# Heads turned from channel rows to token rows by VectorE squares of 32 and transfers through DRAM, in both layers

## The chip, the core and the metric

The program runs on one core of a Trainium2 chip. The metric is the device time of one execution in microseconds (us); before the change it is 2276.68 us, the median of three runs (2275.68 to 2278.51). The engines are TensorE (PE, and PEld for its weight loads), VectorE (DVE), ScalarE (ACT), GpSimd (POOL) and SyncE (SP), which here issues every transfer (DMA).

## What is computed

One step of a two-layer decoder for a prompt of 1024 tokens and for 8 sample tokens. Layer 0 has 8 gated DeltaNet heads and 8 mLSTM heads, layer 1 has 4 GLA heads and 4 retention heads. Cut to what matters:

```python
def _even_mixer(h, ...):                       # layer 0
    proj = h @ w_in
    u_conv = causal_conv(u_a); q_a, k_a, v_a = split(silu(u_conv))
    q_a, k_a = _l2n(q_a) * DK_A ** -0.5, _l2n(k_a)
    o_a, new_gdn = _gated_delta(q_a, k_a, v_a, beta, g_a, s_gdn)   # S_new = e^last S + k^T (e^(last-b) U)
    h_b, ... = _mlstm(q_b, k_b, v_b, ig, fg, ...)                  # C_new = se C + (k we)^T v
    h_b = sigmoid(o_pre) * _rms(h_b, mlstm_norm_w)
    y = concat([_rms(o_a), h_b]) * silu(z)
    return y @ w_out, ...

def _odd_mixer(h, ...):                        # layer 1
    o_c, new_gla = _gla(q_c, k_c, v_c, g_c, s_gla)                 # o += att @ v
    o_d, new_ret = _retention(rotary(q_d), rotary(k_d), v_d, s_ret)
    y = concat([_rms(o_c), _rms(o_d)]) * silu(z)
    return y @ w_out, ...
```

The projections give every head with its channels in the partitions and the 1024 tokens along the row. A product that sums over tokens, such as the state's update, needs its operands with tokens in the partitions. Turning them is what this case is about.

## The kernel before, in words

The prompt is cut into 8 chunks of 128 tokens. A projection of 128 columns (`proj`) multiplies the weights, split into a high and a low part (`whi`, `wlo`), with the input, split likewise (tiles `s_h`), in 72 passes of 344 columns into three PSUM banks `pj`. Weights are loaded into one of two buffers `wf` (512 KB each), ScalarE writes `whi`, and VectorE or GpSimd writes `wlo`. The out projections at the end of each layer first split the 16 rows of `y` in the same way, through the staging tiles `s_pt` and `s_u`, into tiles that the layer's last heads leave free; two late rows (14 and 15) come last in the sums.

Everything is recorded first and then put in order by `Recorder.order`, a planner: it takes each operation's cost and dependences from formulas in the code (`_cost`, `_pe_cost`) and writes one fixed order for every engine and for SP's issues. So an edit to one helper moves instructions everywhere. All operations have the same source line in the profile (L448, where the planner emits them), and groups are told apart by the names of their tiles.

In layer 0 a DeltaNet head (`gdn_mix`) waits for `k2`, `v2` and `q2`, which `conv_silu` makes in this order from three projections. Before the change it turns `k2` by eight TensorE transposes into two PSUM banks (`transpose4`), from which ScalarE takes squares (tile `N`, whose row sums normalise the keys) and VectorE the decayed keys `kd`. It turns `v2` likewise into `vs`. Then come the matrix `N` (products of `k2` with itself), its inverse (tiles `EM`, `Y`, with round trips through the DRAM tiles `nd` and `yd`), and a chain over the 8 chunks, in which `kd` and `vs` are read. `k2`, `kd`, `vs` and `N` have one buffer each. An mLSTM pair (`mlstm_pair_mix`) turns `mk` into `kwe`, an mLSTM head (`mlstm_mix`) turns its value `v` (in one of three buffers `pt`) into `va`, and `mlstm_out` turns the normalised output `hn` (tile `mp`) back. Transposes are 128 x 128, in groups of four to a bank.

In layer 1 both kinds of heads turn two values of 128 channels in `v_tokens`, by `by_token`: sixteen VectorE transposes each of 32 partitions by 256 elements, which need neither TensorE nor a transfer. `by_token` also turns the keys there.

## Time and profile before

| | |
|---|---|
| median of three runs | 2276.68 us |
| the profiled execution | 2275.8 us, of which the span from the first to the last instruction is 2273.7 us |
| TensorE matmuls | 2206.5 us busy, 97% of the span |
| VectorE | 1379.6 us, 61% |
| ScalarE | 745.8 us, 33% |
| GpSimd | 604.7 us, 27% |
| transfers | 236.10 MB, 104 GB/s on average |

Busy time is a union, so overlapped instructions count once. The mean duration of a matmul is that of one from its issue to its modelled end; neighbours overlap, and the time that a matmul holds TensorE is the step from its start to the start of the next one. Layer 0's heads run from about 150 to 1165 us of the span, its out projection to about 1330 us, layer 1's heads to about 2050 us.

### The profile page before, as it was taken

To read this page: it belongs to the slowest core of one execution; us is meant where nothing else is said; L and a number is where in the kernel's file an instruction comes from. 1 tells how busy PE (TensorE), PEld (TensorE's weight loads), DVE (VectorE), ACT (ScalarE), POOL (GpSimd) and SP (SyncE) were. 2 spreads that over 40 slices of the span, in tenths; PEclk is the share of its full clock that TensorE was granted. 3 is DMA by queue.
4 is the path that set the end of the run, shared out by engine and by line. 5 is a ranking of instruction groups with operands and counts; after the bars stand their busy time and mean duration, and the time that the engine had idled before them with its cause. 6 is when DMAs were issued, how large, how long until landed. Compare 5 with 4: busy or idle time off the path is not lost.

```text
span 2273.7 us, 42794 instructions
## 1 busy us (share of the span) xinstructions
PE 2206.5 (97%) x17820; PEld 2056.0 (90%) x17820; DVE 1379.6 (61%) x2771; ACT 745.8 (33%) x1374; POOL 604.7 (27%) x409
## 2 busy tenths in 40 slices
PE   6989999999999999999989999999999999998998
PEld 4867788899998999899989999999999999998997
DVE  6764646566475746647452356785885885886322
ACT  4422323232233223232331134234225324334322
POOL 3221211212123102221330032533532642643210
PEclk9999999999999999999999999999999999999999
DMA  9363453523133223433273221233143143155212
GB/s 261 122 150 81 144 151 83 162 53 93 46 111 103 76 60 87 103 95 84 93 221 93 75 86 38 59 122 104 49 133 96 48 134 104 45 170 191 75 56 94
DMA packets 285944, 236.10 MB, mean 104 GB/s; under 512 B 47803, under 2 KB 258229, under 8 KB 285742
## 3 DMA queue, kind: packets, MB, share of 16 engines
q1 hardware_dynamic: 285750, 233.37, 35.7%
q8 instruction: 140, 2.29, 0.4%
q14 instruction: 54, 0.44, 0.1%
HBM read 186.35 MB, written 47.18 MB: 103 GB/s over the span
## 4 chain that ended last, share of the span: by engine, by line
PE 87%; DVE 5%; DMA 5%; issue 1%; SPq 1%; ACT 1%; POOL 0%; POOLq 0%; DVEq 0%; ACTq 0%
PE pj L448 68%; PE A L448 14%; PE B L448 5%; SPq L448 1%; DMA wf<-in_ev_w_in 1%; DMA wf<-in_ada_w 1%; DMA yd<-s_EM 1%; DVE wlo L448 1%; DMA s_h<-in_x_prompt 1%; DVE s_EM L448 0%; DVE arena L448 0%; DVE s_N L448 0%; DVE s_tmp L448 0%; DMA s_EM<-yd 0%; DVE s_zz L448 0%
## 5 line engine op out<-in xcount | busy, mean ns | idle before, releaser
L448 PE MATMUL pj<-s_h,whi 128*128 128x344 f32 (+1 forms) x6024 | 1498.6, 327 | 9.8 <-ACT whi L448 3.8
L448 PEld LDWEIGHTS pj<-s_h,whi 128*128 128x128 f32 (+1 forms) x6024 | 1043.6, 189 | 40.5 <-issue 22.9
L448 PE MATMUL pj<-s_h,wlo 128*128 128x344 f32 (+1 forms) x3024 | 985.0, 326 | 0.3 <-DVE wlo L448 0.3
L448 PEld LDWEIGHTS pj<-s_h,wlo 128*128 128x128 f32 (+1 forms) x3024 | 571.2, 189 | 19.5 <-issue 15.4
L448 DVE TENSOR_TENSOR wlo<-wf,whi 128x1024 fp32r<-128x1024 f32 x112 | 145.7, 1301 | 259.3 <-ACT whi L448 235.9
L448 ACT ACTIVATE whi<-wf 128x1024 fp32r<-128x1024 f32 (+1 forms) x146 | 152.3, 1043 | 380.3 <-PE pj L448 308.9
L448 ACT ACTIVATE s_pt<-pj 128x344 f32<-128x344 f32 (+1 forms) x170 | 77.0, 453 | 276.0 <-PE pj L448 271.5
L448 POOL TENSOR_TENSOR wlo<-wf,whi 128x1024 fp32r<-128x1024 f32 (+1 forms) x32 | 79.9, 2497 | 179.8 <-ACT whi L448 179.8
L448 POOL TENSOR_TENSOR arena<-arena,base 128x8 f32<-128x8 f32 (+5 forms) x38 | 59.9, 1580 | 240.1 <-DVE arena L448 240.1
L448 POOL TENSOR_TENSOR s_tmp<-s_EM 128x512 f32<-128x512 f32 (+1 forms) x60 | 91.6, 1540 | 100.3 <-DVE s_N L448 32.1
L448 DVE SCALAR_TENSOR_TENSOR arena<-arena,A 128x128 f32<-128x128 f32 (+1 forms) x84 | 32.9, 391 | 111.3 <-PE A L448 111.2
L448 DVE SCALAR_TENSOR_TENSOR s_pt<-s_u,base,s_pt 128x1024 f32<-128x1024 f32 x72 | 96.7, 1343 | 0.5
L448 ACT ACTIVATE s_u<-pj 128x344 f32<-128x344 f32 x93 | 41.6, 452 | 140.6 <-PE pj L448 70.7
L448 POOL TENSOR_TENSOR s_tmp<-s_tmp,arena 128x1024 f32<-128x1024 f32 (+2 forms) x26 | 46.7, 1808 | 124.9 <-PE A L448 66.0
L448 DVE SCALAR_TENSOR_TENSOR s_zz<-s_pt,pj 128x344 f32<-128x344 f32 x96 | 48.5, 505 | 24.4 <-ACT s_pt L448 23.5
L448 DVE SCALAR_TENSOR_TENSOR arena<-arena,B 64x130 f32<-64x130 f32 (+1 forms) x84 | 31.1, 370 | 51.0 <-PE B L448 49.9
L448 POOL TENSOR_TENSOR s_kd<-s_kd,s_vs 128x1032 f32<-128x1032 f32 x8 | 19.3, 2411 | 160.0 <-ACT s_vs L448 142.8
L448 ACT ACTIVATE arena<-A,arena 128x128 f32<-128x128 f32 x64 | 23.4, 366 | 107.3 <-PE A L448 107.3
L448 DVE STREAM_TRANSPOSE s_kd<-s_u 32x256 f32<-32x256 f32 x128 | 55.8, 436 | 3.9 <-ACT s_u L448 1.7
L448 POOL MEMSET s_u<- 128x3 f32 x24 | 2.4, 100 | 206.8 <-DVE s_pt L448 197.5
L448 DVE TENSOR_TENSOR s_EM<-s_EM 64x15 f32<-64x15 f32 (+7 forms) x240 | 49.2, 205 | 13.5 <-DMA s_EM<-nd 7.7
L448 DVE STREAM_TRANSPOSE s_vs<-s_v 32x256 f32<-32x256 f32 x128 | 55.7, 435 | 1.9
(643 smaller groups left out, 3665.7 us busy)
## 6 DMA issues: line engine op xcount, KB each, us to landing
wf<-in_ev_w_in SPq DMA_DIRECT2D x64, 512.0 KB
wf<-in_od_w_in SPq DMA_DIRECT2D x48, 512.0 KB
wf<-in_ada_w SPq DMA_DIRECT2D x32, 512.0 KB
s_pt<-yd SPq DMA_DIRECT2D x24, 516.0 KB
s_tmp<-sd SPq DMA_DIRECT2D x24, 512.0 KB
yd<-s_qg SPq DMA_DIRECT2D x15, 516.0 KB
wf<-in_ev_w_out SPq DMA_DIRECT2D x14, 512.0 KB
wf<-in_od_w_out SPq DMA_DIRECT2D x14, 512.0 KB
```

Source lines behind the costliest of these rows:

```text
L448: op.fn(*[self.placed(x) for x in op.args], **{k: self.placed(x) for k, x in op.kw.items()})
```

## The change

A new helper `squares(y, x, z)` turns a head. One VectorE transpose turns all squares of 32 by 32 of the 128 x 1024 tile at once and writes them into a scratch tile `y`; one transfer writes that to one of four DRAM tiles `td` (512 KB); four transfers, one for each group of 32 partitions, read it back into a tile `z` in pieces of 256 elements, so that each square lands in its place. The result is a view of `z` whose elements stand in another order in the row, and the operation that follows puts them in order as it reads.

In layer 0 this takes the place of every `transpose4` and of the transposes in `mlstm_out`: twice for each DeltaNet head, once for each mLSTM pair, twice for each mLSTM head, 36 times in all. The operations behind it read SBUF where they read PSUM: one multiply of 1024 elements for `kd` and for `vs` instead of two of 512, one ScalarE square and one ScalarE copy (`va`) of 1024, four fused multiplies of 256 in `mlstm_out` instead of two of 512. In layer 1 `v_tokens` calls `squares` for its 16 values, followed by a ScalarE copy; the keys there stay with `by_token`. The planner's cost of a VectorE transpose becomes a function of its size.

```diff
-    def transpose4(self, src, g):
-        p = self.ps()
-        for c in range(4):
-            o = 512 * g + 128 * c
-            self.tr(p[:, 128 * c:128 * c + 128], src[:, o:o + 128])
-        return p
...
+        ksq = self.squares(kd.rearrange("p c d -> p (c d)"), k2, self.slot("N", name="ksq"))
+        V.tensor_tensor(in_4(kd), ksq, by_c(self.g_kdec[:, :, h]), op=ALU.mult)
+        self.act(ksq, ksq, AF.Square)
...
+        z = self.squares(vs.rearrange("p c d -> p (c d)"), v2, v2)
+        V.tensor_tensor(in_4(vs), z, by_c(kk[:, 2, :]), op=ALU.mult)
...
+        z = self.squares(kwe.rearrange("p c x d -> p (c x d)"), self.mk, qs)
...
+        z = self.squares(va.rearrange("p c d -> p (c d)"), v, v)
         G.memset(va[:, :, 128:130], 1.0)
-        for g in range(2):
-            t = self.transpose4(v, g)
-            self.act(va[:, 4 * g:4 * g + 4, 0:128], t.rearrange("p (c d) -> p c d", d=128), AF.Copy)
+        self.act(va[:, :, 0:128].rearrange("p c (a j) -> p c a j", j=32), z, AF.Copy)
...
+        z = self.squares(self.slot("va", name="ht"), hn, hn)
+        y4 = y[:, 0:T].rearrange("p (c a j) -> p c a j", c=NC, a=4)
+        for i in range(4):
+            V.scalar_tensor_tensor(y4[:, :, i, :], z[:, :, i, :], self.nw[:, 1:2], y4[:, :, i, :], op0=ALU.mult,
+                                   op1=ALU.mult)
...
+    def squares(self, y, x, z):
+        dma = self.nc.sync.dma_start
+        y, z = y[:, 0:T], z[:, 0:T]
+        self.nc.vector.transpose(y.rearrange("p (b c j) -> p b c j", b=4, c=NC),
+                                 x[:, 0:T].rearrange("p (c b i) -> p b c i", b=4, c=NC))
+        d = self.td[self.turn("td", 4)]
+        dma(d, y)
+        for b in range(4):
+            dma(z[32 * b:32 * b + 32].rearrange("i (a x) -> i a x", a=4),
+                d.rearrange("(a i) (b x) -> b i a x", a=4, b=4)[b])
+        return z.rearrange("p (a c j) -> p c a j", a=4, c=NC)
+
     def v_tokens(self, v):
...
-            t = self.slot(tag, [128, NC, 128], name="vt")
-            self.by_token(t, v[i])
-            vt.append(t)
+            t = self.slot(tag, name="vt")
+            z = self.squares(t, v[i], v[i])
+            self.act(t[:, 0:T].rearrange("p (c a j) -> p c a j", c=NC, a=4), z, AF.Copy)
```

How the order moves, at three places. First TensorE in layer 0, as DeltaNet head 3 begins: `pj` rows are projections, `A_...<-base,s_k` and `A_...<-base,s_v` are transposes of `k2` and `v2` (with the identity, in `base`). Before:

```order
L448 MATMUL pj_111<-s_h_723,whi_107 128x344
L448 MATMUL pj_111<-s_h_703,wlo_109 128x344
L448 MATMUL A_113<-base,s_k_63 128x128 x4
L448 MATMUL A_114<-base,s_k_63 128x128 x4
L448 MATMUL A_115<-base,s_v_65 128x128 x4
L448 MATMUL pj_112<-s_h_443,whi_106 128x344
```

Here twelve transposes stand between two banks of a projection. The same place in the changed kernel, where `A_...<-s_k` is the product of `k2` with itself:

```order
L448 MATMUL pj_111<-s_h_727,whi_107 128x344
L448 MATMUL pj_111<-s_h_707,wlo_109 128x344
L448 MATMUL A_113<-s_k_63 128x128
L448 MATMUL A_114<-s_k_63 128x128
L448 MATMUL A_115<-s_k_63 128x128
L448 MATMUL pj_112<-s_h_447,whi_106 128x344
```

The transposes are gone, and products that stood behind them have moved up. In the whole program TensorE's order has 14434 matmuls before and 14146 after, 288 fewer (288 = 36 times 8).

Second SP, which issues transfers in order, between the end of DeltaNet head 2 (its state is stored to `out_p_gdn`) and the middle of head 3; `wf` are weight loads. Before:

```order
L448 DMA out_p_gdn<-arena 128x128
L448 DMA out_p_conv<-arena 3x128
L448 DMA out_s_conv<-arena 8x128
L448 DMA wf_104<-in_ev_w_in 128x8x128
L448 DMA out_p_mc<-arena 64x128
L448 DMA out_p_mn<-arena 64x1
L448 DMA wf_105<-in_ada_w 128x1024
L448 DMA wf_104<-in_ada_w 128x1024
L448 DMA wf_105<-in_ev_w_in 128x8x128
```

A weight load stands here behind short stores alone. The same place in the changed kernel:

```order
L448 DMA out_p_gdn<-arena 128x128
L448 DMA td_129<-s_kd_66 128x1024
L448 DMA wf_104<-in_ev_w_in 128x8x128
L448 DMA rd_128<-s_Y_72 4x258
L448 DMA wf_105<-in_ada_w 128x1024
L448 DMA arena<-in_state_gdn_conv 24x128
L448 DMA out_p_conv<-arena 3x128
L448 DMA out_s_conv<-arena 8x128
L448 DMA s_N_70<-td_129 32x4x256 x4
L448 DMA s_Y_72<-rd_128 128x1032
L448 DMA wf_105<-in_ev_w_in 128x8x128
```

One weight load now stands behind the write of a square, which waits for VectorE's transpose, and one behind the four reads, which wait for that write to land.

Third VectorE, where layer 1's last head meets the out projection: `s_zz<-s_pt,pj` finish the last two projections, `s_mq<-s_pt,s_EM` and `s_va<-s_pt,s_mk` are low parts of rows of `y`, which the out projection needs. Before:

```order
L448 STREAM_TRANSPOSE s_kd_12163<-s_u_79 32x8x32 x7
L448 SCALAR_TENSOR_TENSOR s_zz_10696<-s_pt_83,pj_110 128x344
L448 STREAM_TRANSPOSE s_kd_12163<-s_u_79 32x8x32 x4
L448 TENSOR_TENSOR wlo_109<-wf_105,whi_107 128x1024
L448 SCALAR_TENSOR_TENSOR s_zz_10696<-s_pt_83,pj_111 128x344
...
L448 STREAM_TRANSPOSE s_vs_12426<-s_v_12191 32x8x32 x8
L448 SCALAR_TENSOR_TENSOR s_zz_81<-s_pt_84,pj_111 128x344
L448 STREAM_TRANSPOSE s_vs_12426<-s_v_12191 32x8x32
L448 TENSOR_TENSOR s_aT_11683<-B_117,arena 128x512
L448 TENSOR_TENSOR s_mq_18166<-s_pt_82,s_EM_18105 128x1032
```

The first low part stands behind the small transposes and behind the last piece of the last projection. In the changed kernel:

```order
L448 TENSOR_TENSOR s_mq_17736<-s_pt_82,s_EM_17725 128x1032
L448 STREAM_TRANSPOSE s_vs_12190<-s_v_12094 128x1024
L448 STREAM_TRANSPOSE s_kd_12069<-s_u_79 128x1024
L448 SCALAR_TENSOR_TENSOR s_zz_10604<-s_pt_83,pj_112 128x344
L448 SCALAR_TENSOR_TENSOR s_zz_10604<-s_pt_83,pj_110 128x344
L448 TENSOR_TENSOR s_va_17803<-s_pt_82,s_mk_17792 128x1032
L448 TENSOR_TENSOR wlo_109<-wf_105,whi_107 128x1024
L448 SCALAR_TENSOR_TENSOR s_zz_10604<-s_pt_83,pj_111 128x344
L448 SCALAR_TENSOR_TENSOR s_zz_81<-s_pt_84,pj_112 128x344
```

Two large transposes stand where 32 small ones stood, and two low parts have moved ahead of the last projections' ends.

## Rows read from the trace of the kernel before

**Rows 1.** The page's busy time, share of the span and instructions of each engine

```profile
PE 2206.5 (97%) x17820; PEld 2056.0 (90%) x17820; DVE 1379.6 (61%) x2771; ACT 745.8 (33%) x1374; POOL 604.7 (27%) x409
```

**Rows 2.** The page's chain that ended last, shares of the span by engine

```profile
PE 87%; DVE 5%; DMA 5%; issue 1%; SPq 1%; ACT 1%; POOL 0%; POOLq 0%; DVEq 0%; ACTq 0%
```

**Rows 3.** Busy time by stretch; columns: length, PE, PEld, DVE, ACT, POOL, clock, DMA share, GB/s

```profile
150.00:1100.00 950.00, 935.58 (x7824) 851.43 (x7820) 565.43 (x1381) 280.06 (x583) 184.19 (x143) 1.00 0.36 96
...
1400.00:2000.00 600.00, 599.98 (x5562) 573.37 (x5561) 457.67 (x713) 220.46 (x340) 256.57 (x140) 1.00 0.30 89
2000.00:2100.00 100.00, 91.81 (x644) 87.85 (x643) 75.25 (x124) 43.23 (x61) 38.97 (x16) 0.95 0.56 187
...
2054.00:2065.00 11.00, 5.41 (x21) 4.91 (x21) 10.80 (x19) 5.94 (x7) 4.70 (x2) 0.53 0.70 231
```

**Rows 4.** Groups by form, TensorE transposes; columns: count, busy us, mean ns, idle

```profile
L448 PE MATMUL B<-base,s_mp 128*128 128x128 f32 x80 | 12.5, 277 | 0.0
...
L448 PE MATMUL B<-base,s_pt 128*128 128x128 f32 x64 | 9.7, 274 | 0.0
L448 PE MATMUL A<-base,s_v 128*128 128x128 f32 x64 | 9.6, 273 | 0.0
...
L448 PE MATMUL A<-base,s_k 128*128 128x128 f32 x64 | 8.6, 274 | 0.0
...
L448 PE MATMUL B<-base,s_mk 128*128 128x128 f32 x32 | 4.9, 272 | 0.0
```

**Rows 5.** Timeline of TensorE round five transposes; columns: start, duration, instruction, count

```profile
546.29 0.71 PE L448 MATMUL B<-base,s_pt 128*128 128x128 f32 x5
546.76 0.56 PE L448 MATMUL pj<-s_h,whi 128*128 128x344 f32 x2
547.16 0.32 PE L448 MATMUL pj<-s_h,wlo 128*128 128x344 f32 x1
547.32 0.48 PE L448 MATMUL pj<-s_h,whi 128*128 128x344 f32 x2
```

**Rows 6.** Groups by form, VectorE transposes; columns as in group 4

```profile
L448 DVE STREAM_TRANSPOSE s_vs<-s_v 32x256 f32<-32x256 f32 x128 | 55.7, 435 | 1.9
...
L448 DVE STREAM_TRANSPOSE s_EM<-s_EM 128x256 f32<-128x256 f32 x16 | 7.1, 442 | 10.5 <-DMA s_EM<-yd 10.3
```

**Rows 7.** A 512 KB read, issue and first use, and SP's waits for 512 KB writes

```profile
1111.37 0.33 SPq L448 DMA_DIRECT2D s_mp<-gd  x1
...
1115.04 2.49 POOL L448 TENSOR_TENSOR s_mp<-arena,s_mp 128x1024 f32<-128x1024 f32 x1 [1.52 <-DMA s_mp<-gd]
...
SPq L448 <- DMA out_s_gdn<-s_tmp: 9.5, 4, 3.4
```

**Rows 8.** Timeline of VectorE and TensorE, DeltaNet head 3

```profile
496.52 1.22 DVE L448 SCALAR_TENSOR_TENSOR s_k<-s_pt,s_pt 128x1032 f32<-128x1032 f32 x1
...
513.37 1.23 DVE L448 SCALAR_TENSOR_TENSOR s_q<-s_pt,s_pt 128x1032 f32<-128x1032 f32 x1 [1.21 <-ACT s_pt L448]
...
579.91 0.48 PE L448 MATMUL A<-arena,s_kd 128*128 128x128 f32 x2
```

**Rows 9.** Timeline of SP and ScalarE, one weight load and its use

```profile
597.58 0.38 SPq L448 DMA_DIRECT2D wf<-in_ev_w_in  x1
...
608.20 1.06 ACT L448 ACTIVATE whi<-wf 128x1024 fp32r<-128x1024 f32 x1 [3.16 <-PE pj L448]
```

**Rows 10.** TensorE's waits from 2000 to 2100 us, and VectorE there

```profile
PE pj L448 <- ACT s_mk L448: 3.6, 1, 3.6
PE pj L448 <- DVE s_va L448: 2.5, 1, 2.5
...
2042.52 3.58 DVE L448 STREAM_TRANSPOSE s_vs<-s_v 32x256 f32<-32x256 f32 x8
```

**Rows 11.** TensorE, transposes of the last mLSTM output and the first use of that row

```profile
1158.63 1.03 PE L448 MATMUL B<-base,s_mp 128*128 128x128 f32 x8
...
L448 PE MATMUL pj<-s_mp,s_zz x3: 318/320/322, 1208.2 to 1210.1; 128*128 128x344 f32 x3
```

More of the change, by code (lines that the diff above doesn't have):

```diff
@@ L116, in _cost @@
         if method == "transpose":
-            return 436.0, False
+            return 100 + 1.31 * n, False
         if method == "tensor_tensor_scan":
@@ L1218, in gdn_mix @@
         vs = self.slot("vs", [128, NC, L], name="vs")
-        for g in range(2):
-            p = self.transpose4(v2, g)
-            V.tensor_tensor(vs[:, 4 * g:4 * g + 4, :], p.rearrange("p (c d) -> p c d", d=L),
-                            kk[:, 2, 4 * g:4 * g + 4].unsqueeze(2).to_broadcast([128, 4, L]), op=ALU.mult)
+        z = self.squares(vs.rearrange("p c d -> p (c d)"), v2, v2)
+        V.tensor_tensor(in_4(vs), z, by_c(kk[:, 2, :]), op=ALU.mult)
         em = self.slot("EM", [128, NC, L], name="EM")
@@ L1435, in mlstm_pair_mix @@
         kwe = self.slot("kwe", [128, NC, 2, 64], name="kwe")
-        for g in range(2):
-            t = self.transpose4(self.mk, g).rearrange("p (c x d) -> p c x d", c=4, x=2)
-            for x in range(2):
-                V.tensor_tensor(kwe[:, 4 * g:4 * g + 4, x, :], t[:, :, x, :],
-                                self.g_we[:, 4 * g:4 * g + 4, 2 * p + x].unsqueeze(2).to_broadcast([128, 4, 64]),
-                                op=ALU.mult)
+        qs = self.slot("qs", [128, T], name="qs")
+        z = self.squares(kwe.rearrange("p c x d -> p (c x d)"), self.mk, qs)
+        for x in range(2):
+            V.tensor_tensor(kwe[:, :, x, :].rearrange("p c (a j) -> p c a j", j=32), z[:, :, 2 * x:2 * x + 2, :],
+                            self.g_we[:, :, 2 * p + x].unsqueeze(2).unsqueeze(3).to_broadcast([128, NC, 2, 32]),
+                            op=ALU.mult)
         self.kwe = kwe
-        qs = self.slot("qs", [128, T], name="qs")
         for x in range(2):
@@ L1478, in mlstm_mix @@
         va = self.slot("va", [128, NC, 130], name="va")
+        z = self.squares(va.rearrange("p c d -> p (c d)"), v, v)
         G.memset(va[:, :, 128:130], 1.0)
-        for g in range(2):
-            t = self.transpose4(v, g)
-            self.act(va[:, 4 * g:4 * g + 4, 0:128], t.rearrange("p (c d) -> p c d", d=128), AF.Copy)
+        self.act(va[:, :, 0:128].rearrange("p c (a j) -> p c a j", j=32), z, AF.Copy)
         V.tensor_copy(self.vs[:, x, :], v[:, T:W])
@@ L1541, in mlstm_out @@
         y = oz
-        for g in range(2):
-            t = self.ps()
-            for i in range(4):
-                self.tr(t[:, 128 * i:128 * i + 128], hn[:, 4 * g + i, :])
-            s = slice(512 * g, 512 * g + 512)
-            V.scalar_tensor_tensor(y[:, s], t, self.nw[:, 1:2], oz[:, s], op0=ALU.mult, op1=ALU.mult)
+        hn = hn.rearrange("p c d -> p (c d)")
+        z = self.squares(self.slot("va", name="ht"), hn, hn)
[3 more added lines that the diff above has]
+                                   op1=ALU.mult)
         V.tensor_copy(self.ozs[:, h % 2, :], oz[:, T:W])
@@ L1712, in v_tokens @@
         for i, tag in enumerate(("kd", "vs")):
-            t = self.slot(tag, [128, NC, 128], name="vt")
-            self.by_token(t, v[i])
-            vt.append(t)
+            t = self.slot(tag, name="vt")
+            z = self.squares(t, v[i], v[i])
+            self.act(t[:, 0:T].rearrange("p (c a j) -> p c a j", c=NC, a=4), z, AF.Copy)
+            vt.append(t[:, 0:T].rearrange("p (c d) -> p c d", c=NC))
         return vt
@@ L2142, in build @@
             self.rd = [dr.tile([4, QB], F32, name=f"rd{i}") for i in range(2)]
+            self.td = [dr.tile([128, T], F32, name=f"td{i}") for i in range(4)]
             self.nyd = {x: [dr.tile([64, 528], F32, name=f"{x}{i}") for i in range(2)] for x in ("nd", "yd")}
```

10 lines of the change are left out of this document (3 added, 7 removed).

## The prediction

> **What bounds the kernel now.** I read the page's busy shares first: TensorE is busy for 97% of the span, VectorE for 61%, ScalarE for 33%, GpSimd for 27% [rows 1]. Then the chain that ended last: 87% of it lies on TensorE, 5% each on VectorE and transfers [rows 2]. A mean over stages may mislead, so I cut the span: from 150 to 1100 us, where layer 0's heads run, TensorE idles for 950 - 935.6 = 14.4 us; from 1400 to 2000 us, in layer 1's heads, for 0.02 us although VectorE is busy for 457.7 of the 600 us; from 2000 to 2100 us, where layer 1's heads meet its out projection, for 8.2 us [rows 3]. So a matmul taken away in layer 0 is worth its own time there, unless something new makes TensorE wait; VectorE work taken away in the middle of layer 1 is worth nothing; and the seam at 2050 us is the one place where VectorE's work may count.
>
> **TensorE's transposes in layer 0, removed.** There are 288 (36 uses of eight). Their groups show a busy time of 9.7, 9.6, 8.6, 4.9 and, for `mp`, 64 of 80 instances of 12.5, which is 10.0: 42.8 us [rows 4]. That counts each one's tail over its neighbour, so it is an upper end. The step between starts is the better price: five transposes start at 546.29 and the next pass at 546.76, 0.47 us; the two passes after them take 0.40 us to 547.16, where the step of one is otherwise 0.16 (547.16 to 547.32), so 0.08 more is lost in the change [rows 5]. Five cost 0.47 to 0.55 us, 0.094 to 0.11 each. I take 0.112, since most stand in groups of four and five and each group pays that change: 288 x 0.112 = **32 us**, ends 27 and 43.
>
> The trace gives a transpose a mean duration of 272 to 277 ns [rows 4], but neighbours overlap, so that is no price. The Trainium skill, in "TensorE: Matmul & The Clock Gate", Part 4: PE-mode transpose, tells of about 275 ns for one in a kernel's context; the trace agrees with that duration, but a sum that used it as a price, 288 x 0.275 = 79 us, would be an estimate from that page and reach 2198 us, which the steps between starts speak against.
>
> **What takes their place, in layer 0.** Each of the 36 squares is one VectorE transpose of 128 x 1024, one write, four reads. The trace has VectorE transposes only of 256 elements: 435 ns on 32 partitions, 442 ns on 128 [rows 6], so width is free and four times that, 1.77 us, is an upper end; a VectorE operation of 128 x 1032 at 1.22 us [rows 8] is the lower. I take 1.5, nearer the first as a fixed part is counted once. For 512 KB, a read took from its issue at 1111.37 to its first use at 1115.04, 3.7 us, and SP waited for a 512 KB store at most 3.4 us [rows 7]. So a square takes 1.5 + 3.7 + three more issues of 0.33 + 3.7 = about **10 us** where the transposes took one or two. Whom does that delay?
> - The keys: in head 3, `k2` is complete at 496.52 + 1.22 = 497.7, `q2` only at 514.6 [rows 8], since two more projections lie between. The square lands at about 508, the row sums some 3 us later. What needs `q2` waits for it longer. `kd` itself is first read at 579.9 [rows 8], and `vs` is first read in that chain too. Both are covered by the projection and the inverse. Without that cover each us would count once for each of eight heads, since `k2` has one buffer and the next head starts when the chain ends.
> - The last mLSTM output: before, its transposes stand at 1158.6 and that row of `y` is first used at 1208.2 [rows 11]; 10 us more, and as many for its value `v`, fit into 49.
> - VectorE: 36 x 1.5 = 54 us more over about 1000 us, from 60% of the time [rows 3] to 65%. The multiplies behind it are about as long as before and I set them to nothing: they read 1024 elements once instead of 512 twice.
> - SP: 36 x 5 issues of about 0.33 us are 59 us. What matters is the place: weight loads now stand behind a square's write and reads. A load was issued at 597.58 and first used at 608.20 [rows 9]; with 3.7 us of transfer it had 6.9 us to spare.
>
> For new waits of TensorE in layer 0 I take **+4 us**, between 0 (layer 1 shows VectorE at 76% with no wait) and +15 (the idle time doubles) [rows 3]. The nearer row is the first.
>
> **Layer 1.** Each head drops 32 x 0.435 = 13.9 us of VectorE [rows 6] and gets 2 x 1.5; for eight heads 87 us of VectorE go, and 16 ScalarE copies of about 1.06 us (as the `whi` copy [rows 9]) come. From 1400 to 2000 us this buys nothing. At the seam it may: TensorE waits there for VectorE's `va` (2.5 us) and ScalarE's `mk` (3.6 us), while VectorE still turns the last head's values at 2042.5 [rows 10]. In the new order two low parts of `y` stand ahead of the last projections' ends. At stake are the 8.2 us of idle time, and from 2054 to 2065 us a granted clock of 0.53 after these waits (the 1.2 GHz level for most of it), in which 5.4 us of matmuls would have taken half [rows 3]: 8.2 + 2.7 = 10.9. But ScalarE's two copies come in the same place, and the staged rows must still arrive. I take **-5 us**, ends +2 and -11.
>
> **Sum**, against the profiled execution: span 2273.7 - 32 - 5 + 4 = 2240.7; its own time is 2.1 us above its span and the median 0.9 above that: 2243.7, rounded to **2243 us**.
>
> **Rivals.**
> - *VectorE stands at the landings.* Its queue is in order, and each multiply or copy behind a square waits for four reads; behind it may stand the chunk chain's state updates and the low parts of weights, for which TensorE waits. If each of 36 squares costs 0.5 us of TensorE that way, it is +18: 2261 us. For it: 36 new waits. Against it: the fixed order puts other work between, and VectorE has over a third of its time free.
> - *Weight loads are held up: slower than before.* SP issues in order. A load behind a square's write waits for VectorE's transpose, one behind its reads for the write's landing (3.7 us). The place is the SP order at each head's start. It costs 36 x (hold - 6.9 us): nothing up to a hold of 6.9, as much as is gained (34 us) at 7.8; at 8.5 it gives 2243 + 58 = 2301 us. Against it: 3.7 us is well below 6.9, so VectorE would have to be 4 us late at most squares.
> - *The upper ends.* The busy time of the transposes (43) and the whole seam (11) go, and nothing new is waited for: 2276.7 - 54 = 2223 us. The PSUM banks that transposes held speak for it, the steps between starts against it.
> - *The reads are slow for their layout.* If a square's four reads took 30 us instead of 4.7, `k2`'s square would end at 533, after `q2`; about 20 us more in each of eight chains give 2243 + 160 = 2403 us. It decides from about 13 us, at which each chain is 4 us longer. The Trainium skill, in "VectorE: DVE Perf Modes", The three transpose paths, warns of transfers that transpose by strides, 19 times slower than the crossbar's; no transfer of before shows that, and here the transposing is VectorE's: the reads move runs of 256 elements.
>
> That nothing is removed is no rival: the order has 288 matmuls fewer.
>
> **How the numbers follow.** The forecast's own range is 2228 to 2252, from the ends of the three terms taken together in part; I give it 0.70. The standing VectorE 0.13, the held weights 0.08, the upper ends 0.07, the slow reads 0.02. The range that should hold 8 in 10 goes from 2226 to 2262: it takes in the standing VectorE and leaves out the slower cases and the lowest. Within 0.2% (4.6 us, about what a measurement can tell from no change) lies only a part of the second and third case: faster 0.87, same 0.04, slower 0.09.
>
> **What would show it.** Between 150 and 1100 us the same work should end some 30 us earlier, with TensorE idle for 14 to 25 us in layer 0's heads and no wait for `kd`, `vs`, `va` or `kwe` above 2 us. VectorE transposes of 128 x 1024 should last 1.2 to 1.8 us. In DeltaNet heads `kd` should be ready before `q2`'s product. In layer 1's heads VectorE's busy share should fall from 76% to about 65% with TensorE as full as before, and the idle time near the last seam should shrink. Wrong would be: new waits of TensorE for weights (`whi`, `wlo`) that follow a late load, waits for a landing of `td`, or a step between transposes and passes that was overlapped anyway, so that layer 0 shortens by less than 20 us without new idle time.

## The result and the profile after

The changed kernel takes 2263.47 us (median of five runs, 2253.58 to 2266.17) where the kernel before takes 2277.69 (2275.68 to 2278.51): a ratio of 0.9933, 95% interval 0.9915 to 0.995, so 14 us less, and 20 us more than forecast. Its profiled execution takes 2262.3 us, 2260.1 of it the span.

The page of the changed kernel, busy shares and the chain by engine:

```profile
PE 2179.5 (96%) x17532; PEld 2031.2 (90%) x17532; DVE 1300.5 (58%) x2559; ACT 761.7 (34%) x1374; POOL 587.3 (26%) x409
...
PE 65%; DMA 9%; DVE 5%; ACT 1%; SPq 1%; issue 1%; POOL 0%; POOLq 0%; DVEq 0%; ACTq 0%
```

TensorE is busy for 27 us less than in [rows 1], but the span shrank by 13.6 only. The shares of this chain add up to 82%, because it can be followed back only to 387 us of the span; so its 65% can't be set beside the 87% of [rows 2] as it stands. From 400 to 1167 us, where layer 0's heads end, the chain of before lies on TensorE for 654 and on transfers for 35, that of the changed kernel on TensorE for 427 and on transfers for 173. There something else now often ends last, mostly a transfer.

Busy time by stage, first of the kernel before, then of the changed one: layer 0's heads, its out projection with all that follows up to layer 1's first projection, and layer 1 (columns as in [rows 3]).

```profile
44.90:1169.70 1124.80, 1100.15 (x8891) 997.52 (x8891) 684.45 (x1605) 352.12 (x730) 239.63 (x191) 0.99 0.39 105
1169.70:1367.40 197.70, 192.03 (x1205) 189.69 (x1205) 77.17 (x142) 44.44 (x71) 25.76 (x26) 0.98 0.32 99
1367.40:2261.80 894.40, 885.85 (x7440) 848.85 (x7440) 589.06 (x968) 324.95 (x532) 324.89 (x171) 0.99 0.31 94
```

```profile
42.90:1167.40 1124.50, 1078.94 (x8634) 978.78 (x8634) 711.04 (x1631) 351.58 (x715) 238.73 (x190) 0.98 0.52 138
1167.40:1358.80 191.40, 187.40 (x1174) 185.37 (x1174) 75.92 (x143) 43.70 (x70) 26.55 (x26) 0.98 0.35 104
1358.80:2248.30 889.50, 883.98 (x7441) 847.14 (x7440) 484.59 (x728) 342.19 (x548) 307.58 (x171) 1.00 0.38 114
```

Layer 0's heads are as long as before, 1124.5 us, though 257 matmuls fewer stand in them: 21.2 us less of busy time, 20.9 us more of idle time. The DMA share rose from 0.39 to 0.52.

TensorE's longest waits in layer 0's heads, before and after (columns: total us, times, longest):

```profile
PE A L448 <- DVE s_EM L448: 3.0, 5, 0.9
PE A L448 <- issue: 2.7, 2, 1.6
PE pj L448 <- DMA wf<-in_ada_w: 2.6, 1, 2.6
```

```profile
PE B L448 <- DMA s_tmp<-in_state_mlstm_c: 6.0, 2, 4.5
PE pj L448 <- DMA wf<-in_ada_w: 4.4, 2, 3.7
PE A L448 <- DVE s_N L448: 3.3, 2, 2.5
PE A L448 <- DVE arena L448: 3.2, 1, 3.2
...
PE pj L448 <- DVE s_zz L448: 3.0, 1, 3.0
...
PE B L448 <- ACT s_va L448: 2.4, 2, 2.0
```

No single resource stands out; many waits of 2 to 4.5 us have come. One of them as it happens, on VectorE, then TensorE, then SP (timeline; in brackets the wait and what ended it):

```profile
1094.78 0.35 DVE L448 SCALAR_TENSOR_TENSOR arena<-A,arena,s_vs 128x128 f32<-128x128 f32 x1 [0.53 <-PE A L448]
1099.55 0.88 DVE L448 SCALAR_TENSOR_TENSOR s_zz<-s_mp,base,s_zz 128x256 f32<-128x256 f32 x2 [4.42 <-DMA s_mp<-td]
1100.35 0.34 DVE L448 SCALAR_TENSOR_TENSOR arena<-arena,A 128x128 f32<-128x128 f32 x1
```

```profile
1100.75 0.49 PE L448 MATMUL A<-arena,s_k 128*128 128x128 f32 x2 [3.21 <-DVE arena L448]
```

```profile
1090.68 1.80 SPq L448 DMA_DIRECT2D s_mp<-td  x4
```

VectorE's multiply in `mlstm_out` stands for the square of `hn`, whose four reads SP issued from 1090.68; behind it in VectorE's queue stands the DeltaNet state update, and TensorE needs that state. This is the first rival's picture.

A wait can cost twice. TensorE's stretch round the wait for `s_tmp<-in_state_mlstm_c` (after the columns for the five engines: the granted clock):

```profile
929.90:934.30 4.40, 0.00 (x0) 0.00 (x0) 3.79 (x19) 0.00 (x0) 0.00 (x0) 1.00 0.87 225
...
935.00:938.40 3.40, 3.40 (x14) 3.34 (x15) 1.20 (x9) 0.72 (x1) 1.90 (x1) 0.51 0.23 30
```

After 4.4 us of idle time, 3.4 us run at about half clock (1.2 GHz): 1.7 us lost behind the wait. Not every wait has this after it: behind the 3.21 us above, from 1100.7 to 1110 us, the granted clock is 1.00. The record of the granted clock shows such stretches in both traces; TensorE was busy at the lower clock in layer 0 and its out projection for 25.4 us before and 44.1 us after.

### The profile page after: what moved, and what is told of

Read it like the earlier page. It is cut to its first block, busy times and chain, and to the rows that moved or that the text cites. A ratio compares the mean times of both kernels' runs of the same rounds, so it can differ in the third digit from the quotient of the medians.

```text
span 2260.1 us, 42483 instructions
## 1 busy us (share of the span) xinstructions
PE 2179.5 (96%) x17532; PEld 2031.2 (90%) x17532; DVE 1300.5 (58%) x2559; ACT 761.7 (34%) x1374; POOL 587.3 (26%) x409
## 4 chain that ended last, share of the span: by engine, by line
PE 65%; DMA 9%; DVE 5%; ACT 1%; SPq 1%; issue 1%; POOL 0%; POOLq 0%; DVEq 0%; ACTq 0%
PE pj L448 51%; PE A L448 10%; PE B L448 3%; DMA s_pt<-yd 1%; SPq L448 1%; DMA td<-s_va 1%; DMA s_tmp<-sd 1%; DMA nd<-s_N 1%; DVE wlo L448 1%; DVE s_tmp L448 1%; DMA s_mp<-td 1%; DMA s_qs<-gd 1%; DVE s_EM L448 0%; DMA s_qg<-gd 0%; DVE s_zz L448 0%
## 5 line engine op out<-in xcount | busy, mean ns | idle before, releaser
L448 DVE TENSOR_TENSOR wlo<-wf,whi 128x1024 fp32r<-128x1024 f32 x112 | 154.1, 1376 | 187.1 <-ACT whi L448 182.0
L448 POOL TENSOR_TENSOR s_tmp<-s_EM 128x512 f32<-128x512 f32 (+1 forms) x60 | 81.4, 1370 | 80.6 <-DVE s_N L448 29.3
L448 POOL TENSOR_TENSOR s_tmp<-s_tmp,arena 128x1024 f32<-128x1024 f32 (+2 forms) x26 | 43.4, 1673 | 81.8 <-PE A L448 37.7
L448 ACT ACTIVATE s_tmp<-s_tmp 128x1024 f32<-128x1024 f32 (+1 forms) x44 | 46.3, 1058 | 38.9 <-POOL s_tmp L448 35.6
L448 DVE TENSOR_TENSOR s_tmp<-s_k,s_tmp 128x512 f32<-128x512 f32 (+1 forms) x32 | 43.5, 1361 | 23.8 <-ACT s_tmp L448 23.4
```

The costliest lines, as they stand in the source:

```text
L448: op.fn(*[self.placed(x) for x in op.args], **{k: self.placed(x) for k, x in op.kw.items()})
```

## How the kernels are compared

For layer 0's heads and its out projection I take three numbers from each trace: idle time of TensorE (length less busy time of the two stages above); loss to the clock (half the busy time at 1.2 GHz); and work (busy time less that loss). Before, idle time is 24.65 + 5.67 = 30.3, the loss 12.7, the work 1292.2 - 12.7 = 1279.5. The three come from one profiled execution of each run, which lies within 5 us of the run's median but for e12 (6 us below it), e13 (8 above) and e8 (15 above). Times are medians; each ratio is to runs of before in the same comparison, whose median moved between 2271.8 and 2277.7 us. So us below are the ratio's, times 2276.

| run | median us | ratio (95%) | work | idle | clock loss |
|---|---|---|---|---|---|
| before | 2277.7 | 1 | 1279.5 | 30.3 | 12.7 |
| changed | 2263.5 | 0.9933 (0.9915-0.995) | 1244.3 | 49.5 | 22.1 |
| e1 layer 0 alone | 2256.0 | 0.9928 (0.9905-0.9951) | 1244.0 | 37.7 | 18.8 |
| e2 layer 1 alone | 2265.5 | 0.9963 (0.9948-0.9979) | 1280.4 | 27.9 | 8.9 |
| e3 nothing turned in layer 0 | 2251.7 | 0.9903 (0.9878-0.9928) | 1239.2 | 41.6 | 17.2 |
| e4 read elsewhere | 2249.8 | 0.9898 (0.9872-0.9925) | 1247.3 | 35.1 | 20.1 |
| e5 changed again | 2262.6 | 0.9934 (0.9908-0.996) | 1244.6 | 51.0 | 20.4 |
| e6 changed, reordered | 2250.1 | 0.9885 (0.9863-0.9907) | 1243.8 | 38.9 | 22.6 |
| e7 before, reordered | 2269.0 | 0.9974 (0.9959-0.9989) | 1276.2 | 21.1 | 12.0 |
| e8 squares booked longer | 2288.3 | 1.0061 (1.0035-1.0086) | 1241.0 | 68.2 | 43.3 |
| e9 before, transposes left out | 2274.7 | 0.9987 (0.997-1.0004) | 1248.6 | 49.6 | 21.9 |
| e10 changed, no transfers | 2225.1 | 0.9775 (0.975-0.98) | 1245.1 | 23.6 | 6.5 |
| e11 changed, no squares | 2218.8 | 0.9748 (0.9723-0.9773) | 1243.2 | 19.8 | 11.4 |
| e12 changed, small transfers | 2230.2 | 0.9797 (0.9773-0.9822) | 1244.8 | 25.0 | 10.9 |
| e13 changed, not waited for | 2238.7 | 0.9854 (0.9827-0.9881) | 1243.0 | 37.7 | 16.8 |
| e14 reordered, small transfers | 2237.4 | 0.9836 (0.9815-0.9857) | 1242.3 | 27.7 | 23.0 |
| e15 large transfers booked longer | 2270.5 | 0.9986 (0.997-1.0002) | 1246.1 | 41.0 | 17.4 |
| e16 before, traffic beside it | 2328.8 | 1.0234 (1.0209-1.0258) | 1279.4 | 70.6 | 29.6 |
| e17 direct | 2432.2 | 1.0689 (1.0665-1.0713) | 1238.5 | 154.8 | 59.1 |
| e18 direct, reordered | 2437.3 | 1.0712 (1.0689-1.0735) | 1236.8 | 155.4 | 59.2 |

## The parts, and the price of the transposes

**e1** keeps the old `v_tokens`, **e2** the old `transpose4` in layer 0's heads (the use for the keys stands for the others):

```diff
-            z = self.squares(t, v[i], v[i])
...
+            self.by_token(t, v[i])
```

```diff
-        ksq = self.squares(kd.rearrange("p c d -> p (c d)"), k2, self.slot("N", name="ksq"))
...
+            p = self.transpose4(k2, g)
```

> The change in layer 0 alone; layer 1's values are turned by the sixteen small VectorE transposes as before. The two traces show layer 0's heads ending only 2.3 us earlier, its out projection 8.6 us earlier, and the rest of the 13.5 us at layer 1's end. Theory (what layer 0 gains it gives back in layer 0 itself, by TensorE's waits for squares that land later than planned and by the lower clock behind these waits): 2266 to 2272 us, and from 145 to 1150 us 30 to 45 us of TensorE idle time in pieces over 0.3 us (before 14.7, changed 37). Rival (the transfers and copies of layer 1 cost something, and layer 0 alone is worth the predicted 28 us): 2245 to 2252 us.

> The change in layer 1 alone; layer 0 keeps TensorE's transposes. Theory: worth what the two traces show beyond layer 0's out projection, 13.5 - 8.6 = 5 us: 2270 to 2275 us, with the middle of layer 1 unchanged. Rival (layer 1 gives the whole of the gain seen and layer 0 nothing): 2262 to 2266 us. Rival (squares in layer 1 cost as much as they bring): 2276 to 2279 us.

Layer 0 alone gave 16 us, layer 1 alone 8, both together 15 (and again 15 in e5): the parts don't add. Each of the two was planned anew, and the next section shows that an order by itself is worth as much as what is missing. e1 fell between its theory and its rival; e2's 2265.5 us stands in a rival's range only because before ran at 2271.8 us in that comparison, and its 8 us are nearer to the theory's 5 than to 13.

**e3** turns nothing in layer 0, and the planner makes a new order:

```diff
-        self.nc.vector.transpose(y.rearrange("p (b c j) -> p b c j", b=4, c=NC),
...
-        return z.rearrange("p (a c j) -> p c a j", a=4, c=NC)
+        return x[:, 0:T].rearrange("p (c a j) -> p c a j", c=NC, a=4)
```

> Prices the 288 TensorE transposes by themselves: in layer 0 nothing is turned at all, neither by TensorE nor by squares; the multiplies, squares and copies behind read the unturned heads, so that layer 0's numbers are wrong. Layer 1 as before. Theory (the predicted price of 0.112 us each holds and is lost later): before less 27 to 43 us, 2235 to 2251 us, with no more than 20 us of TensorE idle time over 0.3 us from 145 to 1150 us. Rival (the transposes lay beside other work, so that there was less to gain): less than 16 us below before, 2262 us or more, with no new idle time.

Work fell by 40 us, so the work that was priced at 32 is indeed gone; the time fell by 22, because idle time and clock loss rose by 16 although there is no square at all. Neither expectation holds as written.

**e4** reads from an input in place of `td`:

```diff
-                d.rearrange("(a i) (b x) -> b i a x", a=4, b=4)[b])
+                self.a["x_prompt"][0, 0:128, :].rearrange("(a i) (b x) -> b i a x", a=4, b=4)[b])
```

> The changed kernel, but a square's four reads take the same number of bytes in the same pattern from a part of the input x_prompt instead of from the tile just written, so that they need not wait for the write to land; the write is still made. The values that are read are not the turned ones. All VectorE transposes, all transfers and all issues stay, only the round trip is shortened by the write. Theory (the length of a square, 13.5 us in the trace against 10 predicted, is what TensorE waits for): 8 to 18 us below the changed kernel, 2245 to 2255 us, and TensorE's idle time from 145 to 1150 us falls from 37 to 25 us or less. Rival (traffic: 54 MB more crowd out weight loads; or VectorE's 54 us): within 4 us of the changed kernel, 2259 to 2267 us.

The time is the theory's (23 us below before), but the next runs show that another order alone can do as much, and this one was planned anew: the run settles nothing.

## What another order does

**e5** is the changed kernel again. **e6** and **e7** change one number of the planner in the changed kernel and in the one before:

```diff
-            return 450.0 + op.size / op.rate + (2100.0 if op.size > 1 << 18 else 1400.0)
+            return 460.0 + op.size / op.rate + (2100.0 if op.size > 1 << 18 else 1400.0)
...
-                dma = max(dma, t + 450.0) + op.size / op.rate
+                dma = max(dma, t + 460.0) + op.size / op.rate
```

> The changed kernel unaltered, on the chip of the next three, as their measure. The kernel before spread from 2265 to 2282 us over the runs of the last four, and layer 0 alone gave 2256 us, less than the whole change had given (2263). Theory (both parts together are worth no more than layer 0 alone): 14 to 18 us below before, 2254 to 2263 us. Rival (the parts add up to 16 + 6 us, and the first comparison of the changed kernel was a poor one): 2248 to 2253 us.

> The changed kernel, with the planner's time from a transfer's issue to its start set from 450 to 460 ns: the same instructions in another order. The planner's own plan is 2 us longer (2181.2 against 2179.5). Theory (waits stand where this one order happens to leave little room, and another order leaves them elsewhere): between 2250 and 2270 us, with TensorE's idle pieces from 145 to 1150 us at other places, their sum still 25 to 45 us. Rival (the waits belong to the change's own places, squares of given heads): the same time within 3 us and waits at the same tiles.

> The kernel before with the same 10 ns (its plan: 2219.1 against 2220.7 us): what another order alone does where TensorE has the transposes. Theory (the transposes gave the order room): within 4 us of before, with TensorE idle for 10 to 20 us from 145 to 1150 us. Rival (any order may lose or win 10 us): more than 6 us from before.

e5 has its longest waits at the same places as the first trace (the wait for `s_tmp<-in_state_mlstm_c` is 4.6 us long again, that for `wf<-in_ada_w` 3.5 instead of 3.7), so a fixed order gives much the same waits. Ten nanoseconds in the planner move them elsewhere, and that is worth 11 us: e6 takes 2250.1 us, below both kernels and the best version found that computes everything. Before gained 6 us in the same way (3 to 9 by the interval), more than the 4 that I allowed and short of the rival's, so the kernel before depends on its order too. So a difference of under 10 us between two planned orders says little on the change. That the change gains at all is safer: both orders of the changed kernel are faster than both of before, by 9 to 26 us, though two orders each are few. For that reason e9 to e14 and e16 hold an order fixed: the planner orders the whole work, and instructions are dropped, shrunk or added only when it is issued. In their traces each engine's other instructions stand in the order of the kernel that they are made from.

**e8** books each transfer of a square 4 us longer, **e15** every transfer above 256 KB 1.5 us longer:

```diff
-            return 450.0 + op.size / op.rate + (2100.0 if op.size > 1 << 18 else 1400.0)
+            return 450.0 + op.size / op.rate + (2100.0 if op.size > 1 << 18 else 1400.0) + op.late
```

```diff
-            return 450.0 + op.size / op.rate + (2100.0 if op.size > 1 << 18 else 1400.0)
+            return 450.0 + op.size / op.rate + (3600.0 if op.size > 1 << 18 else 1400.0)
```

> The changed kernel with each transfer of a square booked 4 us longer in the planner (write and reads: 8 us a square, more than the 13.5 - 10 us by which they came late), so that what needs a square is put later in the queues that would stand at it. Theory (VectorE, ScalarE and SP stand at late landings): 5 to 12 us below the changed kernel, and no wait of TensorE behind a landing of the DRAM tile td. Rival (the squares' landings are a small part of the new waits; the rest is weight loads and the chunk chains, which have less time between them now): within 4 us of the changed kernel, 10 us of TensorE idle time or more left at weight loads and state updates.

> The changed kernel with every transfer of over 256 KB booked 1.5 us longer in the planner (3.6 us behind the last byte instead of 2.1; loads of weights and of gd rows, writes of squares, stores), its plan 2193.8 us against 2179.5. The traces show these transfers landing 4.3 to 5.1 us after their issue in the median and 6 to 9 us for the slowest tenth, where the plan holds 4.1. Theory (the order has too little room for landings): 8 us or more below the changed kernel, 2240 to 2255 us. Rival (as with the squares alone, room at one place bunches the transfers at another): 2260 us or more.

Both theories fell: e8 became slower than before, and slower than its rival had it too; e15 is no faster than before, as its rival had it. In e8 VectorE stands elsewhere, as its timeline and SP's show:

```profile
908.52 0.33 SPq L453 DMA_DIRECT2D s_qg<-gd  x1
908.95 6.33 SPq L453 DMA_DIRECT2D s_EM<-in_i  x1
```

```profile
910.39 0.44 DVE L453 SCALAR_TENSOR_TENSOR s_zz<-s_mp,base,s_zz 128x256 f32<-128x256 f32 x1
920.32 1.23 DVE L453 TENSOR_TENSOR s_qg<-s_q,s_qg 128x1024 f32<-128x1024 f32 x1 [9.49 <-issue]
```

The row `s_qg` was read from 908.52, and VectorE stood until 920.32 at the multiply that uses it; one issue alone, of 64 KB, held SP for 6.33 us. TensorE waited 8.7 us in that place. The square is in time there, and another read is late. That booked room drew other transfers together is my reading, from this place and two like it (6.7 and 6.4 us of VectorE); it was not tried by itself. In e15 the part that the theory was about did come: layer 0's heads and its out projection take 1304.5 us against 1315.9 in the changed kernel, with 41.0 us of idle time against 49.5. It loses 7 us ahead of them, by a later start, and 16 in layer 1 (905.4 us against 889.5). Why it loses these stays open.

## The order held: where the gain went

**e9** is the kernel before without its 288 transposes; the operations behind them read the unturned heads. `leave` marks operations that are ordered but not issued, `put` changes what the last operation reads when it is issued:

```diff
+        self.nc.leave = True
         for c in range(4):
...
+        self.nc.leave = False
...
+            u3 = k2[:, 512 * g:512 * g + 512].rearrange("p (c d) -> p c d", d=L)
             self.act(ksq[:, 4 * g:4 * g + 4, :], p3, AF.Square)
+            self.put(u3)
```

> The kernel before in its own order, on every engine, with only the 288 TensorE transposes of layer 0 not issued; the operations behind them read the unturned heads from SBUF, so layer 0's numbers are wrong. No new plan, no square. Layer 0's pure TensorE time (busy time, with what the lower clock doubled taken off) fell by 35 to 40 us in the kernels so far, their time by 15 to 26. Theory (the transposes were partly cover: while TensorE turned heads, weight loads, inverses and state updates caught up, and without them it waits for these): 14 to 24 us below before, with TensorE's idle time in layer 0 up by 8 to 16 us. Rival (what is lost is lost by the new plan or by squares): 30 us or more below before, idle time within 5 us of before's.

Work fell by 31 us and the time by 3, less than either expectation. TensorE's first waits there:

```profile
PE A L451 <- DVE arena L451: 10.1, 4, 4.9
PE pj L451 <- DMA wf<-in_ada_w: 6.4, 3, 5.5
PE B L451 <- DVE s_tmp L451: 3.1, 1, 3.1
```

In that order the transposes had covered waits of nearly their own length: idle time rose by 19 us and the clock loss by 9, together nearly as much as the work that went. "A matmul taken away in layer 0 is worth its own time there" does not hold in it, even without anything new to wait for. In an order planned without the transposes (e3) 22 of 40 us came through, so what they cover belongs to the order, and e9's 3 us are what this one order gives.

**e10** to **e13** take the changed kernel's own order apart, in layer 0 alone. e10 drops the transfers, e11 VectorE's large transposes too, e12 shrinks each transfer to 8 elements a row, and e13 sends the reads, in full size, to another DRAM tile, so that nobody waits for them (in this order, e11 as e10 with `leave` set one operation earlier):

```diff
+        self.nc.leave = self.layer == "even"
         dma(d, y)
```

```diff
         dma(d, y)
+        if small:
+            self.nc.ops[-1].args = (d[:, 0:8], y[:, 0:8])
...
+            if small:
+                self.nc.ops[-1].args = (z[32 * b:32 * b + 32, 0:8], d[32 * b:32 * b + 32, 0:8])
```

```diff
+            if self.layer == "even":
...
+                op.args = (e[32 * b:32 * b + 32].rearrange("i (a x) -> i a x", a=4), op.args[1])
```

> The changed kernel in its own order, with the one write and four reads of each of layer 0's 36 squares not issued; what follows reads the unturned heads, so layer 0's numbers are wrong. VectorE's 36 large transposes stay, layer 1 stays. Theory (engines and queues stand at the squares' landings, 13.5 us after their start, and 36 MB more make other landings late): 10 to 18 us below the changed kernel, TensorE's idle time in layer 0 down from 45 to 30 us or less. Rival (the waits come from what the transposes had covered, not from squares): within 6 us of the changed kernel, 40 us or more of idle time.

> As the last, and VectorE's 36 large transposes of layer 0 are not issued either (45 us of VectorE). Theory (VectorE's time itself is covered, as predicted): within 3 us of the last. Rival (VectorE is a bound in stretches of layer 0): 6 us or more below the last.

> The changed kernel in its own order, with layer 0's squares moving only 8 elements a row (1/128 of the bytes of a write, 1/32 of the partitions' rows of a read as before); every issue, every wait for VectorE, every wait of the reads for the write stays, what follows reads the unturned heads, layer 0's numbers are wrong. It tells the bytes (36 MB more, long landings) from the issues and waits in SP's queue. Theory of bytes: near the kernel without these transfers, at most 4 us above it. Rival (SP stands at the waits, and loads behind it are late): at least 6 us above the kernel without these transfers, near the changed kernel.

> The changed kernel in its own order with all the bytes of layer 0's squares, but a square's four reads go to another DRAM tile instead of SBUF, and what follows reads the unturned heads: every issue and every byte is there, nobody waits for the landing of the reads; layer 0's numbers are wrong. Theory (the squares' own landings are late): within 6 us of the kernel without these transfers, 2225 to 2234 us, TensorE's idle time in layer 0 25 us or less. Rival (the bytes make weight loads and rows of gd late): 2250 us or more, idle time of 35 us or more with waits for wf and for operations behind gd reads.

Ratios to before give, from the changed kernel on: 15 us gained; with the reads not waited for 33; with few bytes 46; without transfers 51; without VectorE's part 57. So in this order about 18 us were lost because engines stood at the landings of the squares' reads, 13 more to the bytes (the write's landing, at which SP stands, and the other transfers), 5 to issues and round trips, 6 to VectorE's 45 us. Each ratio is good to 6 us, so the first two steps are clear of the noise and the last two are not. The runs are no strict ladder: e12 waits again for the reads of 24 of the 36 squares, so its 13 us are what the bytes cost less what these waits cost. In the other 12, the keys and the mLSTM pairs, the multiply behind the square reads the unturned `k2` or `mk` itself in e12, and waits for no read. The theory of landings holds, by more than I expected (36 us instead of at most 18 between the changed kernel and e10). e12, 5 us above e10, lies between its theory's 4 and its rival's 6. e13's time lies between its two ranges, its idle time (37.7 us) in the rival's: the bytes act in both ways, the larger part through the squares' own landings. No run issues the squares' transfers from another engine than SP, so what SP's one queue costs by itself stays open.

The same multiply as above in e12, on VectorE and on TensorE:

```profile
1065.20 0.88 DVE L448 SCALAR_TENSOR_TENSOR s_zz<-s_mp,base,s_zz 128x256 f32<-128x256 f32 x2 [2.61 <-DMA s_mp<-td]
```

```profile
1066.39 0.49 PE L448 MATMUL A<-arena,s_k 128*128 128x128 f32 x2 [1.39 <-DVE arena L448]
```

4.42 us became 2.61, and TensorE's 3.21 became 1.39: same order, same issues, fewer bytes. Over layer 0's heads, who waited for the tile `td` (us, times), changed kernel and e12:

```profile
  POOL s_va L448: 64.4, 4
  POOL arena L448: 18.9, 2
  ACT s_va L448: 14.9, 3
  DVE s_zz L448: 10.1, 3
  DVE s_vs L448: 9.3, 4
  DVE s_kd L448: 5.5, 3
```

```profile
  POOL arena L448: 15.5, 1
  ACT s_va L448: 12.1, 3
  DVE s_zz L448: 2.6, 1
...
  DVE s_vs L448: 1.8, 2
```

VectorE stood for 24.9 us, then for 4.4; of the 24.9, the 5.5 at `s_kd` are the keys', whose multiply waits for no read in e12, so 19.4 against 4.4 is the fair pair. GpSimd stood longest: its memset in `va` waits until the write of the square has read that tile. e13 still has this wait (39.4 us) and e12 has none, so part of the 13 us may be GpSimd's; no run tells. SP, too, stood for the writes; its longest such row in the changed kernel:

```profile
SPq L448 <- DMA td<-s_va: 25.3, 10, 5.8
```

Landings, worked out from the trace's landing records (from an issue to the last of the records that its semaphore shows before that semaphore's next issue; layer 0's heads; median and slowest tenth, us):

| | before | changed | e12 |
|---|---|---|---|
| write of a square | | 4.5, 8.1 | 3.0, 6.6 |
| one of its four reads | | 3.4, 6.0 | 2.4, 3.8 |
| weight load `wf<-in_ev_w_in` | 4.4, 5.6 | 4.5, 6.2 | 4.3, 5.7 |

**e14** is e12 in e6's order.

> The reordered changed kernel (2250 us) with layer 0's squares moving only 8 elements a row; layer 0's numbers are wrong. Theory (in every order the bytes cost what the order has no room for): 2222 to 2235 us, so that both orders come together within 6 us once the bytes are gone, and the 12 us between the orders are waits for landings. Rival (orders differ by themselves): 2238 us or more.

The time lies between the two ranges. 37 us against e12's 46: the two orders differ by 9 us without the bytes too, about as much as two ratios can tell apart, so the landings don't explain all that an order is worth. The bytes cost e6's order some 11 us (26 to 37), where they cost the first order 31.

**e16** puts the same bytes beside the kernel before, in its own order, for nobody:

```diff
+            self.beside(src[:, 0:T])
...
+            dma(d, placed(x))
+            for b in range(4):
+                dma(e[32 * b:32 * b + 32].rearrange("i (a x) -> i a x", a=4),
+                    self.a["x_prompt"][0, 0:128].rearrange("(a i) (b x) -> b i a x", a=4, b=4)[b])
```

> The kernel before in its own order, with the bytes of 36 squares moved beside it for nobody: at the end of each group of TensorE transposes the turned tile is also written to a DRAM tile, and four reads of the same pattern go from an input to another DRAM tile. Nobody waits for them. Theory (the squares' own landings): within 6 us of before. Rival (bytes and issues delay the other transfers): 10 us or more above before.

53 us slower, far past the theory and well inside the rival's range: 36 squares' transfers for which an order holds no place cost 1.5 us of time each, in TensorE's idle time (70.6 us) and its clock. The weight loads' median landing is 4.6 us, hardly longer, so the loss is not in the rate; as the five issues at each place also push the loads behind them back, and SP itself stood 18.7 us for such writes to land, the run doesn't part bytes from issues.

**e17** and **e18** try a square with half the bytes and one landing, SBUF to SBUF:

```diff
-        dma(d, y)
         for b in range(4):
-            dma(z[32 * b:32 * b + 32].rearrange("i (a x) -> i a x", a=4),
-                d.rearrange("(a i) (b x) -> b i a x", a=4, b=4)[b])
+            for a in range(4):
+                dma(z[32 * b:32 * b + 32, 256 * a:256 * a + 256], y[32 * a:32 * a + 32, 256 * b:256 * b + 256])
```

> The changed kernel in both layers, with each square sent from SBUF to SBUF: sixteen transfers of 32 partitions by 256 elements (32 KB) straight from the tile that VectorE turned to the tile that is read, in place of the write to DRAM and the four reads. Half the bytes, one landing, but 16 issues of some 0.35 us on SP (5.6 us a square, 290 us over the program) instead of 5. The numbers are right; the planner's plan is 2179.2 us. Theory (landings and bytes): a square gets shorter by about the write's landing of 4.5 us less 3.9 us more of issuing, with 18 MB less in layer 0: 5 to 20 us below the changed kernel, 2243 to 2258 us. Rival (SP's queue becomes the place where loads stand): 2265 us or more, with TensorE waiting for wf.

> The same with the planner's 450 ns set to 460 (plan 2178.8 us): a second order of it. Theory: within 10 us of the first order and below the reordered changed kernel's 2250 us by as much as 5 to 15 us. Rival: no better than 2250 us.

157 and 162 us slower. SP in e17:

```profile
527.92 10.31 SPq L448 DMA_DIRECT2D s_N<-s_kd  x16
538.33 0.49 SPq L448 DMA_DIRECT2D arena<-in_state_gdn_conv  x1
...
539.59 0.41 SPq L448 DMA_DIRECT2D wf<-in_ev_w_in  x1
```

Sixteen issues hold SP for 10.3 us, 0.64 each and not the 0.35 that I took, and a weight load stands behind them. The rival holds in its time; TensorE's waits for `wf` (15.5 us over layer 0's heads) are only part of it.

## The prediction, step by step

- **Transposes removed, -32 (27 to 43): right as work.** Work fell by 35.2 us in the changed kernel (1279.5 to 1244.3), and by 31 to 43 in every kernel without them, 0.11 to 0.15 us each. The cleanest is e9, in before's own order: 30.9 us, 0.107 each. That this work becomes time is another matter, as e9 shows. The Trainium skill, in "TensorE: Matmul & The Clock Gate", Part 4: PE-mode transpose, tells of about 275 ns for one in a kernel's context. As a duration the traces agree (272 to 277 ns [rows 4]); taken as a price it would be twice what these runs show, and the measurement decides.
- **Layer 1, -5: right.** Its stage went from 894.4 to 889.5 us. VectorE there fell from 457.7 us [rows 3] to 371.3 of the same 600, with TensorE as full as before, and between 2028 and 2055 us the granted clock is 1.00, where [rows 3] had 0.53 round that seam:

```profile
1400.00:2000.00 600.00, 599.59 (x5580) 572.96 (x5579) 371.34 (x519) 230.51 (x350) 244.66 (x141) 1.00 0.40 118
```

```profile
2028.00:2055.00 27.00, 22.92 (x160) 21.47 (x159) 15.69 (x32) 12.53 (x15) 14.09 (x6) 1.00 0.95 278
```

- **New waits of TensorE in layer 0, +4 (0 to 15): this step failed.** Idle time rose by 49.5 - 30.3 = 19.2 us and the loss to the clock by 9.4, so +28.6. With -35.2, -5 and 2 us that an earlier start gave, this is the 13.6 us of the spans. What the runs showed in its place: without the squares' transfers the same order has 30.1 us of idle time and clock loss together (e10), less than before's 43.0. So in this order the whole +28.6 comes with the transfers, 18 us of time by engines that stand at landings of reads (e13) and 13 by the bytes (e12). The +4 came from layer 1, where VectorE at 76% made nobody wait; but there the values were turned without a transfer, so that row held no wait for a square's landing. And the clock behind new waits was left out, though [rows 3] had shown it at the seam.
- **The squares, 10 us: right in the middle, with no account of the slow ones.** VectorE's transposes take 1.24 us (1.5 taken):

```profile
L448 DVE STREAM_TRANSPOSE s_vs<-s_v 128x1024 f32<-128x1024 f32 x16 | 19.8, 1235 | 4.4 <-ACT s_v L448 4.3
```

  With the medians of the table, 1.2 + 4.5 + 1.3 of issues + 3.4 = 10.4 us. A square whose write and last read both fall in the slowest tenth takes 1.2 + 8.1 + 1.3 + 6.0 = 16.6. That these late ones decide fits the waits shown above (4.42 us at one square) and was not tried apart. The 13.5 us from a transpose to the first use, which I gave in expectations as a square's length, is no measure of it: it is about 13 with few bytes too, so it tells mostly where the order puts the use.
- **VectorE's 54 us, set to nothing:** 45 us, worth 6 in e11, which the runs can't tell from nothing.
- **The rivals.** "VectorE stands at the landings", 2261 us, has the mechanism of the larger part: e13 prices waits at the reads' landings at 18 us, the 0.5 us for each of 36 squares that it assumed, though ScalarE's and GpSimd's waits go with VectorE's in that run. That its total is so near the measured 2263.5 is partly luck: it adds 18 to 2243, while this order without the transfers runs at 2225 (e10) and the transfers cost it 36. I gave it 0.13 because VectorE has a third of its time free; that share says nothing of where the free time lies. By the rows the held weight loads were a smaller part, TensorE 4.4 us at `wf`; SP stood 25.3 us at the writes from `va` alone, and no run prices what that held back. The reads are not slow for their layout: 3.4 us in the median. The Trainium skill, in "VectorE: DVE Perf Modes", The three transpose paths, warns of transfers that transpose by strides. None of a square's transfers is one, since the reads move runs of 256 elements. The upper ends (2223) came about only with the transfers left out (e10 2225, e11 2219).
- **The range** ended at 2262 and the time is 2263.5: it stopped at that rival's middle, with no room for another order, which was worth 6 us in e7 and 11 in e6. (The sum of 2243.7 rounds to 2244, not 2243; nothing hangs on that.)

## What to carry to other kernels

An instruction removed from the engine that bounds a kernel is worth its own time only as far as its order has nothing else due at that moment: leave it out in the old order first (here 3 of 31 us), then in a new one (22 of 40). A round trip that takes its place is to be priced by its slow landings too, not by one seen in a quiet place, wherever a queue in order stands behind it, and the lower clock that may follow a wait belongs in the price. And where a planner orders everything, compare several orders before a few us are put down to an edit.

## What the runs showed that I had not expected

A change of 10 ns in the planner moved the time by 11 us in one kernel and by 6 in the other. Left-out transposes in layer 0 were worth 3 us in one order (e9) and, with nothing turned either, 57 us beside layer 1's change in another (e11). Sixteen transfers of 32 KB took SP 10.3 us to issue, and one of 64 KB, with several large ones issued just before it, 6.3 us.
